# Longer loads in slots that shrink: an adaptive max-pool that streams 134 MB through one core

## The chip, the cores and the metric

One core of one Trainium2 chip. The metric is the device time of one execution in microseconds, as a median of several; executions of this kernel agree within about 0.2%. Every kernel was compared with the kernel before on the same chip in the same rounds; the experiments ran on four chips, on which the kernel before took 335.85 to 335.92 us. Two other kernels set side by side may have run on different chips. On one core a run is called slow when it lies more than 1.5% above the fastest run of the same kernel; comparisons below use fast runs. The granted clock was 1.0, and TensorE is not used.

## The reference

The input is 32 x 256 rows of 4,096 float32 values; each output is the maximum of 16 neighbouring values, 256 outputs per row.

```python
batch, channels, length = 32, 256, 4096
for i in range(output_size):                 # output_size = 256
    start = int(i * length / output_size)
    end = int((i + 1) * length / output_size)
    result[:, :, i] = np.max(x[:, :, start:end], axis=-1)
```

So 134.2 MB are read and 8.4 MB written, with one comparison per element. Since 4,096 is a multiple of 256, all windows have W = 16 elements (64 bytes), and the whole input is one row of windows, 16,384 of them for each of the 128 partitions.

## The kernel before

Loads go in turn through three slots of 760 windows (48,640 bytes per partition). VectorE reduces each slot into an output tile that stays in SBUF. Only after the last load has been issued are the outputs stored, in three DMAs. The 16,384 windows of a partition are cut in two groups so that the first group's outputs can be stored while the last inputs are still being reduced.

```python
SLOTS = 3
CHUNK = 760
GROUPS = [10 * CHUNK, total - 10 * CHUNK]     # 7,600 and 8,784 windows
CUT = 10 * CHUNK
ring = pool.tile([P, SLOTS, CHUNK * W], fp32, tag="ring", name="ring")
outs = [pool.tile([P, n], fp32, ...) for i, n in enumerate(GROUPS)]   # cut
for g, n in enumerate(GROUPS):
    # cut: xg, og are this group's views of input and output
    for a in range(0, n, CHUNK):
        b = min(a + CHUNK, n)
        slot = ring[:, n_loads % SLOTS, 0 : (b - a) * W]
        n_loads += 1
        nc.sync.dma_start(out=slot, in_=xg[:, a * W : b * W])
        nc.vector.reduce_max(
            out=outs[g][:, a:b],
            in_=slot.rearrange("p (n w) -> p n w", w=W),
            axis=mybir.AxisListType.X,
        )
    # cut: stores of group 0 in one piece, of group 1 in two, cut at CUT
for dst, src in stores:
    nc.sync.dma_start(out=dst, in_=src)
```

Of the kernel before, what the change touches and what calls it, by code (L numbers as in the profile page):

```python
# [1 line left out]

# [4 lines left out]


@with_exitstack
def kernel(  # L10
    ctx: ExitStack,
    tc: tile.TileContext,
    x: bass.AP,
    output_size: bass.AP,
    out: bass.AP,
):




    nc = tc.nc
    P = nc.NUM_PARTITIONS
    fp32 = mybir.dt.float32

    B, C, L = x.shape
    O = int(output_size)
    assert L % O == 0, (L, O)
    W = L // O
    total = B * C * O // P

    SLOTS = 3
    CHUNK = 760
    GROUPS = [10 * CHUNK, total - 10 * CHUNK]
    CUT = 10 * CHUNK
    assert sum(GROUPS) == total and B * C * O % P == 0

    pool = ctx.enter_context(tc.tile_pool(name="pool", bufs=1))
    ring = pool.tile([P, SLOTS, CHUNK * W], fp32, tag="ring", name="ring")
    outs = [
        pool.tile([P, n], fp32, tag=f"out{i}", name=f"out{i}")  # L40
        for i, n in enumerate(GROUPS)
    ]

    xw = x.flatten_outer_dims().rearrange("r (o w) -> (r o) w", w=W)
    ow = out.flatten_outer_dims().rearrange("r o -> (r o)")

    stores = []
    n_loads = 0
    first = 0
    for g, n in enumerate(GROUPS):  # L50
        xg = xw[first : first + P * n].rearrange("(p n) w -> p (n w)", p=P)
        og = ow[first : first + P * n].rearrange("(p n) -> p n", p=P)
        first += P * n
        for a in range(0, n, CHUNK):
            b = min(a + CHUNK, n)
            slot = ring[:, n_loads % SLOTS, 0 : (b - a) * W]
            n_loads += 1
            nc.sync.dma_start(out=slot, in_=xg[:, a * W : b * W])  # L58
            nc.vector.reduce_max(  # L59
                out=outs[g][:, a:b],  # L60
                in_=slot.rearrange("p (n w) -> p n w", w=W),
                axis=mybir.AxisListType.X,
            )
        if g < len(GROUPS) - 1:
            stores.append((og, outs[g]))
        else:
            for a, b in ((0, CUT), (CUT, n)):
                stores.append((og[:, a:b], outs[g][:, a:b]))

    for dst, src in stores:  # L70
        nc.sync.dma_start(out=dst, in_=src)


# [1 line left out]
_INS = ['x', 'output_size']  # L75
_OUTS = [((32, 256, 256), 'float32')]

_NUMBERS = {'output_size': 256}


# [26 lines left out]
```

## Time and profile before

| before | value |
|---|---|
| time, median of 6 runs (range) | 335.86 us (335.66 to 336.07) |
| loads: number, bytes per partition | 21 of 48,640 and 1 of 27,136 |
| period of the loads | 14.38 us |
| one reduction of 760 windows | 12.82 us |
| share of time that the 16 DMA engines are busy | 99.1% |

From the page of the kernel before: the span, the busy time of the engines, the packets and the DMA queue (packets, MB, share of 16 engines' span).

```profile
span 334.0 us, 111 instructions
...
DVE 276.3 (83%) x22; POOL 0.2 (0%) x4
...
DMA packets 3600, 142.61 MB, mean 427 GB/s; under 512 B 400, under 2 KB 400, under 8 KB 528
...
q1 hardware_dynamic: 3600, 142.61, 99.1%
```

VectorE (DVE) is busy for 83% of the time and the DMA engines for 99%. The second number has no room left in it. The timeline shows it from VectorE's side (start, duration, engine, instruction, and in brackets the idle time before it and what ended that):

```profile
61.14 12.82 DVE L59 TENSOR_REDUCE out<-ring 128x760 f32<-128x12160 f32 x1 [1.57 <-DMA ring<-in_x_dram]
75.53 12.82 DVE L59 TENSOR_REDUCE out<-ring 128x760 f32<-128x12160 f32 x1 [1.57 <-DMA ring<-in_x_dram]
89.91 12.82 DVE L59 TENSOR_REDUCE out<-ring 128x760 f32<-128x12160 f32 x1 [1.56 <-DMA ring<-in_x_dram]
```

VectorE works 12.82 us and waits 1.57 us, and every round of the two is 14.38 us. The trace also records each packet: one partition's row of a load is one packet, 48,640 bytes most often in 1.796 us, and each of the 16 engines carries 8 of the 128 rows: 8 x 1.796 = 14.37 us. So a load begins when the one before it ends. The sequencer that issues the loads (SP) waits long for VectorE, in its own view of waits (who waited for whom: total us, times, longest):

```profile
SPq L58 <- DVE out L59: 243.6, 19, 12.8
SPq L58 <- DMA ring<-in_x_dram: 37.2, 19, 15.9
```

That wait is not a loss: while SP waits for a slot, two other loads are still queued at the DMA engines.

### The profile page before, as it was taken

The numbers are of one execution on the slowest core, as the hardware profiler recorded it, in microseconds if no ns is written. First come the engines' busy times: TensorE is split into PE (matmuls) and PEld (weight loads), VectorE is DVE, ScalarE is ACT, GpSimd is POOL, SyncE is SP. The second block draws the span as 40 slices with busy tenths as digits, with TensorE's granted clock in tenths as the row PEclk, the third lists the DMA queues.
The fourth block names the chain that finished last, engine by engine and source line by source line (L and its number), as shares of the span: only waits on it lengthen the run. The fifth ranks groups of instructions, "written<-read, shape, count | busy, mean of one in ns | idle before, by whom it ended". The sixth has DMA issues, their size and how long they took to land.

```text
span 334.0 us, 111 instructions
## 1 busy us (share of the span) xinstructions
DVE 276.3 (83%) x22; POOL 0.2 (0%) x4
## 2 busy tenths in 40 slices
DVE  0088989889898988989898898988989898898990
POOL 0000000000000000000000000000000000000000
DMA  9999899999999999999998999999999999989997
GB/s 361 390 460 454 384 466 437 402 466 437 402 460 425 419 454 408 443 454 396 454 454 384 466 437 402 466 419 419 460 414 431 454 408 443 454 384 440 443 419 306
DMA packets 3600, 142.61 MB, mean 427 GB/s; under 512 B 400, under 2 KB 400, under 8 KB 528
## 3 DMA queue, kind: packets, MB, share of 16 engines
q1 hardware_dynamic: 3600, 142.61, 99.1%
HBM read 134.22 MB, written 8.39 MB: 427 GB/s over the span
## 4 chain that ended last, share of the span: by engine, by line
DMA 68%; DVE 27%; DVEq 2%; SPq 0%; issue 0%
DMA ring<-in_x_dram 68%; DVE out L59 27%; DVEq L102 2%; SPq L58 0%
## 5 line engine op out<-in xcount | busy, mean ns | idle before, releaser
L59 DVE TENSOR_REDUCE out<-ring 128x760 f32<-128x12160 f32 (+1 forms) x22 | 276.3, 12565 | 49.2 <-DMA ring<-in_x_dram 49.2
L88 POOL MEMSET const-bfloat16-1.0<- 128x1 bf16 x1 | 0.1, 101 | 0.0
L88 POOL MEMSET const-uint8-127<- 128x1 uint8 x1 | 0.1, 101 | 0.0
L88 POOL MEMSET const-float32-0.0<- 128x1 f32 x1 | 0.1, 98 | 0.2 <-issue 0.2
L88 POOL MEMSET const-float32-1.0<- 128x1 f32 x1 | 0.1, 98 | 0.0
## 6 DMA issues: line engine op xcount, KB each, us to landing
ring<-in_x_dram SPq DMA_DIRECT2D x21, 6080.0 KB, 30.3
out_dram<-out SPq DMA_DIRECT2D x2, 3800.0 KB, 30.1
ring<-in_x_dram SPq DMA_DIRECT2D x1, 3392.0 KB, 23.9
out_dram<-out SPq DMA_DIRECT2D x1, 592.0 KB, 7.6
```

Of the source, the lines that this page charges most:

```text
L59: nc.vector.reduce_max(out=outs[g][:, a:b], in_=slot.rearrange("p (n w) -> p n w", w=W), axis=mybir.AxisListType.X,)
L88: nc = _bacc.Bacc("TRN2", target_bir_lowering=False, num_devices=1)
L102: with _tile.TileContext(nc) as tc:
```

## The change

The intent is to use all of SBUF at every moment. At the start few outputs exist, so the three slots can be 64 KB per partition; as outputs accumulate, growing down from the top of one common area, the slots shrink round by round to 48 KB. This makes 19 loads of 22, each as long as memory and a cap of 64 KB per partition permit. Each group is loaded from its end backwards.

```diff
-    CHUNK = 760
-    GROUPS = [10 * CHUNK, total - 10 * CHUNK]
+    AREA = 53200
+    MOST = 65536 // (4 * W)
+    ALIGN = 4
+    ROUNDS_A = 3
+    LAST = 4
+    sizes = []
+    left = total
+    while left:
+        room = AREA - (total - left)
+        n = min(room // (SLOTS * W + SLOTS) // ALIGN * ALIGN, MOST)
+        for _ in range(SLOTS):
+            n = min(n, left)
+            if n:
+                sizes.append(n)
+                left -= n
+    groups = [sizes[: ROUNDS_A * SLOTS], sizes[ROUNDS_A * SLOTS :]]
...
-            slot = ring[:, n_loads % SLOTS, 0 : (b - a) * W]
+            at = n_loads % SLOTS * sizes[n_loads // SLOTS * SLOTS] * W
+            slot = area[:, at : at + size * W]
             nc.sync.dma_start(out=slot, in_=xg[:, a * W : b * W])
             nc.vector.reduce_max(
-                out=outs[g][:, a:b],
+                out=area[:, base + a : base + b],
...
-            for a, b in ((0, CUT), (CUT, n)):
-                stores.append((og[:, a:b], outs[g][:, a:b]))
+            end = sum(loads[len(loads) - LAST :])
+            for a, b in ((end, n), (0, end)):
+                stores.append((og[:, a:b], area[:, base + a : base + b]))
```

The loads become three each of 1,024, 980, 924, 868, 816 and 768 windows and one of 244.

More of the change, by code (lines that the diff above doesn't have):

```diff
@@ L29 @@
     total = B * C * O // P
+    assert B * C * O % P == 0
+    AREA = 53200
     SLOTS = 3
-    CHUNK = 760
-    GROUPS = [10 * CHUNK, total - 10 * CHUNK]
-    CUT = 10 * CHUNK
-    assert sum(GROUPS) == total and B * C * O % P == 0
-    pool = ctx.enter_context(tc.tile_pool(name="pool", bufs=1))
-    ring = pool.tile([P, SLOTS, CHUNK * W], fp32, tag="ring", name="ring")
-    outs = [
-        pool.tile([P, n], fp32, tag=f"out{i}", name=f"out{i}")
-        for i, n in enumerate(GROUPS)
-    ]
+    MOST = 65536 // (4 * W)
[13 more added lines that the diff above has]
+    groups = [sizes[: ROUNDS_A * SLOTS], sizes[ROUNDS_A * SLOTS :]]
+    pool = ctx.enter_context(tc.tile_pool(name="pool", bufs=1))
+    area = pool.tile([P, AREA], fp32, tag="area", name="area")
     xw = x.flatten_outer_dims().rearrange("r (o w) -> (r o) w", w=W)
@@ L49 @@
     first = 0
-    for g, n in enumerate(GROUPS):
+    low = AREA
+    for g, loads in enumerate(groups):
+        n = sum(loads)
         xg = xw[first : first + P * n].rearrange("(p n) w -> p (n w)", p=P)
@@ L53 @@
         first += P * n
-        for a in range(0, n, CHUNK):
-            b = min(a + CHUNK, n)
-            slot = ring[:, n_loads % SLOTS, 0 : (b - a) * W]
-            n_loads += 1
+        base = low - n
+        b = n
+        for i, size in enumerate(loads):
+            a = b - size
+            at = n_loads % SLOTS * sizes[n_loads // SLOTS * SLOTS] * W
+            slot = area[:, at : at + size * W]
             nc.sync.dma_start(out=slot, in_=xg[:, a * W : b * W])
             nc.vector.reduce_max(
-                out=outs[g][:, a:b],
+                out=area[:, base + a : base + b],
                 in_=slot.rearrange("p (n w) -> p n w", w=W),
@@ L63 @@
             )
-        if g < len(GROUPS) - 1:
-            stores.append((og, outs[g]))
-        else:
-            for a, b in ((0, CUT), (CUT, n)):
-                stores.append((og[:, a:b], outs[g][:, a:b]))
+            n_loads += 1
+            b = a
+        low = base
+        if g == 0:
+            stores.append((og, area[:, base : base + n]))
+        else:
+            end = sum(loads[len(loads) - LAST :])
+            for a, b in ((end, n), (0, end)):
+                stores.append((og[:, a:b], area[:, base + a : base + b]))
     for dst, src in stores:
```

## The prediction

> # Prediction
>
> **What bounds the kernel now.** The 16 DMA engines, from end to end. The page shows one queue keeping them busy for 99.1% of a 334.0 us span: 142.61 MB at 427 GB/s. VectorE is busy 276.3 us (83%); after each 12.82 us reduction it waits 1.56 us for a load, and loads come every 14.38 us (timeline). The trace's packet records show no gap over 0.03 us on any engine from the first load's packet (2.0 us into the span) to the last store's (1.1 us before its end). A row of a load is one packet: 48,640 bytes take 1.796 us, and 8 per engine make 14.37 us, the loads' period. So VectorE's 49.2 us of idle time (waits) costs nothing, nor do the 243.6 us that load issues wait for slots (the queue's own waits): two more loads are always queued.
>
> **What the change moves.** Bytes stay: 134.22 MB in, 8.39 MB out. The order view of the builds shows 22 loads becoming 19 (three each of 65,536, 62,720, 59,136, 55,552, 52,224 and 49,152 bytes per partition, one of 15,616). Data packets per engine fall from 200 to 176, if a 64 KB row stays one packet, and semaphore packets (9 ns each) from 25 to 22.
>
> **Cost of a packet.** 27,136 bytes take 1.009 us and 48,640 bytes 1.796 us: 36.6 ns per 1,000 bytes and 13.5 ns fixed, of which 3 ns overlap the next packet. Estimate from these: 24 x 10.6 ns + 3 x 9 ns = 0.28 us saved. A 64 KB packet should take 2.41 us, its load 19.3 us, the reduction of 1,024 windows 17.3 us (12.82 x 1024/760), so VectorE keeps up and the queue stays fed.
>
> The Trainium skill, "DMA: Bandwidth & Descriptors", section "Anatomy of one DMA", fits about 2.0 us of fixed cost to every DMA. Paid here, three loads fewer would save 6 us. This trace disagrees: a period of 14.38 us against 14.37 us of packets leaves 0.01 us per load; a queued DMA hides its fixed part behind its predecessor.
>
> **Ends.** The first load must still begin at 2.0 us; its first packets took 2.3 to 3.1 us instead of 1.8, and I expect a similar extra. The last store grows from 0.6 to 1.3 MB and waits for the last reduction. Estimate: the last 768-window load lands at 309 us, its reduction ends at 322, the 244-window one (4.1 us) at 326; the store's packets are ready at 327.5, while the two stores ahead (10.4 and 6.0 us) keep the engines busy until 330. Slack 2 us, so no bubble. The last two stores' rows no longer begin at multiples of 64 bytes: 0 to 0.2 us.
>
> **Prediction: 335.6 us**, range 335.0 to 336.2: within 2% (0.985), faster 0.003, slower 0.012. Larger loads gain about 0.1%, as the pipe was already full.
>
> **What would show each step.** DMA share of 99% again; 3,168 packets (2,432 for loads, 384 for stores, 352 for semaphores); 64 KB packets at 2.41 us; VectorE waiting 2 us per load in the first rounds, 1.5 in the last; VectorE busy within 0.5 us of 276; no DMA gap before the last store.
>
> **What would make it wrong.** A 65,536-byte row cut in two (+0.1 us at most) or moved at another rate; loads waiting for a later reduction than the third back, since slots now overlap at shifted places, so that the queue runs dry at round changes; a drained queue before the last store (some 2 us); unaligned store rows at a multiple of their time (stores carry 19 us per engine, so 10% is 2 us).

## The result, and the profile after

| | before | after |
|---|---|---|
| time, median of 6 runs (range) | 335.86 us (335.66 to 336.07) | 335.67 us (335.42 to 335.87) |
| ratio of the fast runs | | 0.9993, interval 0.998 to 1.0006 |
| time, repeated on another occasion (9 and 5 runs) | 335.86 us (335.64 to 336.1) | 335.53 us (335.42 to 335.77) |

A ratio is the mean time of one kernel's fast runs over that of the other's in the same rounds, so it is not quite the ratio of the medians in the table. The time lies inside the predicted range of 335.0 to 336.2 us and 0.07 us from the predicted 335.6. The change makes no difference that these intervals can tell from none; both pairs of medians lean the same way, by 0.19 and 0.33 us.

The page after:

```profile
span 333.9 us, 109 instructions
...
DVE 276.0 (83%) x19; POOL 0.2 (0%) x4
...
DMA packets 3168, 142.61 MB, mean 427 GB/s; under 512 B 352, under 2 KB 352, under 8 KB 352
...
q1 hardware_dynamic: 3168, 142.61, 99.1%
```

There are 432 packets fewer and the same bytes, the same share and the same rate. A 64 KB row is one packet (3,168 = 19 x 128 + 3 x 128 for data and 22 x 16 for semaphores). The timeline after, over a change of round:

```profile
42.33 17.22 DVE L75 TENSOR_REDUCE area<-area 128x1024 f32<-128x16384 f32 x1 [2.13 <-DMA area<-in_x_dram]
61.68 17.22 DVE L75 TENSOR_REDUCE area<-area 128x1024 f32<-128x16384 f32 x1 [2.13 <-DMA area<-in_x_dram]
80.28 16.49 DVE L75 TENSOR_REDUCE area<-area 128x980 f32<-128x15680 f32 x1 [1.38 <-DMA area<-in_x_dram]
98.72 16.49 DVE L75 TENSOR_REDUCE area<-area 128x980 f32<-128x15680 f32 x1 [1.96 <-DMA area<-in_x_dram]
```

Everything is stretched in proportion: the period is 19.35 us (8 packets of 2.418 us), the reduction 17.22 us. The first wait of a new round is shorter (1.38 us) only because a shorter load follows a longer reduction; no later slot is waited for. SP's waits:

```profile
SPq L74 <- DVE area L75: 246.2, 16, 17.2
SPq L74 <- DMA area<-in_x_dram: 38.8, 16, 20.9
```

Three loads fewer, and in total nearly the same waiting as before (285.0 us against 280.8 us). It is still not on the path.

### The profile page after: what moved, and what is told of

The parts are those of the page before. It is cut to its first block, busy times and chain, and to the rows that moved or that the text cites. A ratio compares the mean times of both kernels' runs of the same rounds, so it can differ in the third digit from the quotient of the medians.

```text
span 333.9 us, 109 instructions
## 1 busy us (share of the span) xinstructions
DVE 276.0 (83%) x19; POOL 0.2 (0%) x4
## 2 busy tenths in 40 slices
DMA packets 3168, 142.61 MB, mean 427 GB/s; under 512 B 352, under 2 KB 352, under 8 KB 352
## 3 DMA queue, kind: packets, MB, share of 16 engines
q1 hardware_dynamic: 3168, 142.61, 99.1%
## 4 chain that ended last, share of the span: by engine, by line
DMA 63%; DVE 34%; another core or an unknown queue 1%; issue 0%; SPq 0%
DMA area<-in_x_dram 63%; DVE area L75 34%; SPq L74 0%
## 5 line engine op out<-in xcount | busy, mean ns | idle before, releaser
L75 DVE TENSOR_REDUCE area<-area 128x1024 f32<-128x16384 f32 (+6 forms) x19 | 276.0, 14525 | 50.0 <-DMA area<-in_x_dram 50.0
```

What stands on the lines that cost most here:

```text
L75: nc.vector.reduce_max(out=area[:, base + a : base + b], in_=slot.rearrange("p (n w) -> p n w", w=W), axis=mybir.AxisListType.X,)
```

## The experiments

The theory: the 16 DMA engines move bytes without a pause, so the size and number of loads count only through a few nanoseconds per packet; whatever a DMA costs besides is hidden behind the DMA ahead of it in the queue. Rivals: each DMA has an exposed cost of microseconds, which another loss happened to cancel; VectorE shares the bound; the end of the kernel or the shifted slots gave back a gain.

Results agreed with the reference except in the two kernels that are wrong on purpose.

### Smaller loads, three slots: more DMAs and more packets

```diff
-    CHUNK = 760
-    GROUPS = [10 * CHUNK, total - 10 * CHUNK]
-    CUT = 10 * CHUNK
+    CHUNK = 190
+    GROUPS = [40 * CHUNK, total - 40 * CHUNK]
+    CUT = 40 * CHUNK
```

> The kernel before with loads a quarter as long: 87 loads of at most 12,160 bytes per partition instead of 22, still three slots. Theory (the queue never drains; a packet costs 10.6 ns beside its bytes, a load only its 9 ns semaphore packet): packets per engine 696 + 24 instead of 176 + 24, so 520 x 10.6 ns + 65 x 9 ns = 6.1 us more, 342.0 us; DMA share stays at 99%. Rival (each DMA pays about 2 us): 65 x 2 us more, about 466 us, with DMA share near 70%.

Measured: 342.44 and 345.52 us in the fast runs, 350.11 and 350.70 in two that count as slow; the kernel before 335.9. The profiled run is one of the slow ones, with its packets and queue:

```profile
DMA packets 12962, 142.63 MB, mean 409 GB/s; under 512 B 1440, under 2 KB 1440, under 8 KB 1696
...
q1 hardware_dynamic: 12960, 142.61, 98.7%
```

The exposed 2 us per DMA are refuted: 130 us did not come. But the theory's 342.0 us was hit only by the fastest run, and executions that differ by 8 us mean that something other than packets varied. The packet records of the profiled (slow) run show gaps of up to 2 us on single DMA engines. (The kept records don't name the engine of a packet; here and below they are joined, end to start, into 16 chains.) That called for two separations: packets from DMAs, and DMAs from the depth of the queue.

### As many packets, no more DMAs

The 22 loads of before, but each partition's part is gathered from four pieces (Q = 4) of 12,160 bytes; outputs and stores follow the same order (cut here).

```diff
-        xg = xw[first : first + P * n].rearrange("(p n) w -> p (n w)", p=P)
+        xg = xw[first : first + P * n].rearrange("(p q n) w -> p q (n w)", p=P, q=Q)
...
-            nc.sync.dma_start(out=slot, in_=xg[:, a * W : b * W])
+            nc.sync.dma_start(
+                out=slot.rearrange("p (q e) -> p q e", q=Q),
+                in_=xg[:, :, a // Q * W : b // Q * W],
+            )
...
```

> The kernel before with its 22 loads, but each partition's part of a load is gathered from four pieces of 12,160 bytes, so that there are as many packets as in the quarter loads and no more loads. Packets per engine: 704 for loads and 72 for stores (two stores come in pieces) instead of 176 and 24. Theory (packets cost, loads do not): 576 x 10.6 ns = 6.1 us more, 342.0 us, equal to the quarter loads within 0.5 us. Rival (the number of DMAs costs): 336 us, as before.

Measured: 338.22 us (338.12 to 338.38) against 335.9. The page:

```profile
DMA packets 12816, 142.61 MB, mean 424 GB/s; under 512 B 400, under 2 KB 912, under 8 KB 1936
...
q1 hardware_dynamic: 12816, 142.61, 99.6%
```

Packets do cost something, 2.3 us for 576 more per engine, but that is 4.0 ns each and not the 10.6 ns of the prediction. And this kernel was not equal to the quarter loads, so those lost their further time elsewhere.

### Smaller loads, six slots

```diff
-    SLOTS = 3
+    SLOTS = 6
     CHUNK = 190
```

> The quarter loads (12,160 bytes per partition, 87 loads) with six slots instead of three. With three slots they varied from 342.4 to 350.7 us, with gaps on single DMA engines; the quarter rows, which never drained, showed only 4 ns per extra packet (2.3 us for 576). Theory (the excess over that was the queue running dry, as two loads of 3.6 us do not cover 3.3 us of reduction, 1.2 to 2.3 us from issue to packet and 1 us between the first and the last engine): with five loads queued 520 x 4 ns + 65 x 9 ns = 2.7 us over the kernel before, 338.6 us, all runs within 0.5 us, no engine gaps. Rival (each of 65 more loads costs 0.1 to 0.2 us whatever is queued): 342 to 350 us as with three slots.

Measured: 339.0 us (338.93 to 339.19) against 335.85. The queue of this kernel:

```profile
DMA packets 12962, 142.63 MB, mean 423 GB/s; under 512 B 1440, under 2 KB 1440, under 8 KB 1696
...
q1 hardware_dynamic: 12960, 142.61, 99.6%
```

With three more slots and nothing else changed, the scatter vanished and the engines were busy 99.6% of the time. So 65 more loads with 520 more packets cost 3.15 us (0.4 us more than expected), which is 0.05 us per load, packets included; after 65 x 9 ns for semaphore packets, 4.9 ns remain per packet. What the three-slot version lost beyond that came from its shallow queue, since depth alone cured it. Its slow profile shows the loss in two forms: per engine 3.0 us of gaps, and 10.1 us by which packets exceed the median time of their size (1.5 us with six slots). Few of those long packets follow a gap, so the gaps alone don't explain the loss. (The two versions ran on different chips, on which the kernel before took 335.9 and 335.85 us.)

### Half the work on VectorE

```diff
-                in_=slot.rearrange("p (n w) -> p n w", w=W),
+                in_=slot.rearrange("p (n w) -> p n w", w=W)[:, :, : W // 2],
```

> The changed kernel with each reduction reading only the first 8 of 16 elements of every window (a wrong result on purpose): VectorE's work halves to about 139 us, the DMAs stay. Theory (DMA engines bound everything): 335.7 us as the changed kernel, within 0.3 us. Rival (VectorE, 83% busy and 34% of the chain that ended last, shares the bound): a gain of several us.

Measured: 335.65 us (335.47 to 335.70) against 335.9, with

```profile
DVE 139.4 (42%) x19; POOL 0.2 (0%) x4
...
q1 hardware_dynamic: 3168, 142.61, 99.1%
```

VectorE's work halved and the time stayed that of the changed kernel. VectorE bounds nothing, although in the page of the changed kernel the chain that ended last gives it 34% of the span.

### Two slots of 64 KB: a candidate that failed

If only bytes and packets count, two slots are enough, and every load can be 64 KB.

```diff
-    SLOTS = 3
-    CHUNK = 760
+    SLOTS = 2
+    CHUNK = 1024
+    TAIL = 252
...
```

Cut: the last load gets a piece of SBUF of its own, and the groups and stores are cut to match.

> A candidate: 15 loads of 64 KB, one of 772 windows and one of 252 in a piece of its own, in only two slots. 17 loads, packets per engine 136 + 24 (200 before, 176 in the changed kernel). Theory: a slot is free 17.2 us after its load lands and the first packet follows its issue by about 1.0 us (0.73 to 1.75 us at the start), together 18.3 us, less than the 19.35 us that the other load takes: queue stays fed, 40 fewer packets than before: 335.86 - 0.45 = 335.4 us, DMA share 99%. Rival (three slots are needed, or DMAs have an exposed cost of about 2 us): a gap of 0.5 to 1 us at each of 14 loads, 343 to 350 us.

Measured: 353.39 us (350.73 to 354.07) against 335.9: slower than the rival expected, and my theory's number failed by 18 us. The timeline:

```profile
42.57 17.22 DVE L64 TENSOR_REDUCE out<-ring 128x1024 f32<-128x16384 f32 x1 [2.33 <-DMA ring<-in_x_dram]
64.00 17.22 DVE L64 TENSOR_REDUCE out<-ring 128x1024 f32<-128x16384 f32 x1 [4.22 <-DMA ring<-in_x_dram]
83.77 17.22 DVE L64 TENSOR_REDUCE out<-ring 128x1024 f32<-128x16384 f32 x1 [2.54 <-DMA ring<-in_x_dram]
104.76 17.22 DVE L64 TENSOR_REDUCE out<-ring 128x1024 f32<-128x16384 f32 x1 [3.77 <-DMA ring<-in_x_dram]
```

```profile
q1 hardware_dynamic: 2880, 142.61, 96.4%
```

VectorE now waits 2.3 to 4.4 us where the changed kernel had 2.13 us at this size, and the DMA share fell. I had allowed 1.0 us from issue to first packet and had left out two things that the packet records show. First, the 16 engines do not work in step: from the first engine's semaphore to the last one's, a load lands over 0.8 us at the start of this run and a median of 2.2 us over all of it. A load counts as landed when the slowest engine is done, while the fast ones already run dry. Second, while other packets are moving, the first packet on an engine that ran dry comes a median of 2.2 us after the issue in this run; and it takes a median of 0.56 us longer than its size demands. Per engine the gaps sum to 7.5 us, and what all packets take above the median of their size sums to 9.7 us (0.85 us in the kernel before): together most of the 17.5 us lost. The packets right after a gap make only about 3.5 us of the 9.7; why others ran long too was not found.

### The same two slots, freed earlier

The two-slot kernel with the halved reduction of above, so that only the moment changes at which a slot becomes free.

```diff
 # on the two-slot kernel
-                in_=slot.rearrange("p (n w) -> p n w", w=W),
+                in_=slot.rearrange("p (n w) -> p n w", w=W)[:, :, : W // 2],
```

> The two-slot kernel with 64 KB loads (353.4 us), each reduction reading half of every window (wrong result on purpose), so that a slot is free after about 8.7 us instead of 17.2 us; DMAs the same. Theory (the two-slot kernel ran dry because the next load was issued too late): the queue is fed again, 335.5 us, DMA share 99%, landing spread of the engines stays near 0.8 us. Rival (two slots or 17 loads of 64 KB are slow by themselves, in the memory or the engines): stays near 353 us.

Measured: 335.61 us (335.49 to 335.75) against 335.85; the landing spread stayed at 0.8 to 0.9 us.

```profile
197.19 8.69 DVE L64 TENSOR_REDUCE out<-ring 128x1024 f32<-128x8192 f32 x1 [10.66 <-DMA ring<-in_x_dram]
216.54 8.69 DVE L64 TENSOR_REDUCE out<-ring 128x1024 f32<-128x8192 f32 x1 [10.66 <-DMA ring<-in_x_dram]
```

The period is 19.35 us again. So neither two slots nor 64 KB rows are slow; the late issue was.

### Two slots of 48 KB

```diff
-    SLOTS = 3
+    SLOTS = 2
     CHUNK = 760
```

> The kernel before with two slots instead of three: 22 loads of 48 KB. Asks what the size of a load is worth when only one load is queued behind the one that moves. In the two-slot kernel with 64 KB loads each load came 1.0 to 1.3 us late (353.4 us, 14 loads with a wait), the spread of the engines rose to 2 us and packets came a median of 2.2 us after their issue. Theory (fed only if the other load's time covers reduction, issue to packet and spread): slack is 14.38 - 12.84 - 2.2 - 0.95 = -1.6 us, against 19.35 - 17.24 - 2.2 - 0.8 = -0.9 us with 64 KB, at 20 loads instead of 14: about 1.5 to 2 us per load, 365 to 375 us. Rival (a late load costs the same few tenths whatever its size, or two slots suffice at 48 KB): under 353 us.

Measured: 355.13 and 357.25 us in the fast runs, 363.21 and 364.08 in the slow ones, against 335.92. The estimate of 365 to 375 us was too high and the rival's bound too low. In the middle of the timeline (138 to 242 us) only every second load is late: VectorE waits 2.7 to 3.2 us, then 1.6 to 1.9.

```profile
152.71 12.82 DVE L59 TENSOR_REDUCE out<-ring 128x760 f32<-128x12160 f32 x1 [1.56 <-DMA ring<-in_x_dram]
168.41 12.82 DVE L59 TENSOR_REDUCE out<-ring 128x760 f32<-128x12160 f32 x1 [2.89 <-DMA ring<-in_x_dram]
```

I had not modelled that. Nor did the 2.2 us that I took over from the last kernel hold: here the first packet on an engine that ran dry came a median of 1.2 us after the issue, though in most rounds all 16 engines were still moving packets when the load was issued. With a queue this shallow, 64 KB loads (median 353.39 us, on another occasion) were better than 48 KB ones by 2 to 4 us in fast runs. The direction is that of the change's intent, but the size is small, and these two kernels scatter too much to say more.

### One slot: what a load costs when nothing hides it

The kernel before, and the quarter loads, each with `SLOTS = 1`.

> The kernel before with one slot: every load waits for the reduction of the load before it, so what a load costs apart from its bytes is laid bare. Estimate: 14.37 us of packets, 0.8 us of slow first packets, 12.82 us of reduction, 1.2 to 2.3 us from issue to packet, 0.3 us from packet to reduction, about 30 us per load, 660 us in all (640 to 680).

> One slot with the quarter loads: same bytes, 65 more loads, all of them exposed. If a load that nothing hides costs 2.0 us beside bytes and reduction, 65 x 2.0 + 8.3 us (reductions) + 2.7 us (packets) over the one-slot kernel, about 800 us; with slow first packets and the spread of the engines counted, about 2.7 us per load, 845 us. With a queue that is fed the same 65 loads cost at most 3 us (six slots).

Measured: 655.99 and 826.72 us (two executions each). One round of each, first with 48 KB loads, then with 12 KB:

```profile
47.96 12.82 DVE L59 TENSOR_REDUCE out<-ring 128x760 f32<-128x12160 f32 x1 [17.06 <-DMA ring<-in_x_dram]
78.13 12.82 DVE L59 TENSOR_REDUCE out<-ring 128x760 f32<-128x12160 f32 x1 [17.35 <-DMA ring<-in_x_dram]
```

```profile
25.78 3.32 DVE L59 TENSOR_REDUCE out<-ring 128x190 f32<-128x3040 f32 x1 [6.07 <-DMA ring<-in_x_dram]
35.16 3.32 DVE L59 TENSOR_REDUCE out<-ring 128x190 f32<-128x3040 f32 x1 [6.07 <-DMA ring<-in_x_dram]
```

A load of 14.37 us of packets keeps VectorE waiting 17.2 us, one of 3.6 us keeps it waiting 6.1 us: some 2.4 to 2.8 us per load beside the bytes. From the totals: 170.7 us more, less 10.0 us of further VectorE work and about 2.3 us of packets (520 x 4.5 ns), over 65 loads, gives 2.4 us per load. So a cost of microseconds per DMA does exist. These 2.4 us hold everything that is exposed: a median of 1.1 us from issue to first packet, a first packet that runs 0.6 to 0.7 us long, and the wait for the last engine. With six slots the same 65 loads cost 0.05 us each.

### The end of the kernel: one store fewer

```diff
-            for a, b in ((end, n), (0, end)):
+            for a, b in ((0, n),):
```

> The changed kernel with its last two stores joined into one, which must wait for the last reduction (326.0 us in the trace of the changed kernel). The first store ends at 323.4 us, and the packets of the joined one come 1.2 to 2.3 us after 326.0, so that the engines idle 4 to 5 us. Theory (in the changed kernel the middle store covers the last reductions): 9.0 us of store from about 327.7 us, 340.0 us in all (339 to 341). Rival (the end is not sensitive; one DMA fewer): 335.6 us.

Measured: 339.19 us (339.04 to 339.22) against 335.86, and 335.53 for the changed kernel on the same chip. DMA share (the second-last column; the last is GB/s) in two stretches of the end, first the changed kernel, then this one:

```profile
300.00:323.00 23.00, 21.39 (x3) 0.00 (x0) 1.00 1.00 431
323.00:329.00 6.00, 3.00 (x1) 0.00 (x0) 1.00 0.96 411
```

```profile
300.00:323.00 23.00, 21.38 (x3) 0.00 (x0) 1.00 0.97 419
323.00:329.00 6.00, 2.77 (x1) 0.00 (x0) 1.00 0.49 208
```

The changed kernel keeps the engines moving while the last 768 and 244 windows are reduced, because the middle store was ready long before. Without it there is a gap of 3.5 to 4.4 us per engine, and the total is 3.7 us longer. The gap was half a microsecond shorter than I expected: with all engines idle the packets came 0.84 to 0.99 us after the issue, not 1.2 to 2.3.

### The changed kernel again

> The changed kernel itself, unaltered, five rounds against the kernel before on the same chip, to narrow the interval of the difference (0.19 us of medians in the first measurement, ratio 0.9993, interval 0.998 to 1.0006). Theory (24 fewer packets per engine at 4 to 5 ns and 3 fewer semaphore packets, less 0.1 us of slower first packets): 0 to 0.2 us faster. If packets saved 10.6 ns as the prediction had it, about 0.3 us faster.

Measured: 335.53 us (335.42 to 335.77) against 335.86 (335.64 to 336.1), ratio 0.9992, interval 0.9979 to 1.0006. This does not tell 0.1 from 0.3 us.

## Why the prediction was right

**The bound.** The prediction placed it in the DMA engines. Halving VectorE's work left the time where it was, and removing the cover of the middle store, hence idling the engines for 3.5 to 4.4 us, cost 3.3 us over the kernel before. A rate within a packet can be read off two sizes: 36,480 bytes lie between the 455 ns of 12,160 bytes and the 1,796 ns of 48,640, which is 36.76 ns per 1,000 bytes, or 27.2 GB/s per engine and about 435 GB/s for 16. The Trainium skill, "DMA: Bandwidth & Descriptors", section "Where 436 GB/s comes from", derives 435.2 GB/s. A rival would be a limit that the engines share, such as the memory; packets should then be shorter when few engines move. They are not: in the one-slot quarter loads 95 packets of 12,160 bytes have at most eight packets moving at their middle, and their median is 455 ns too. So the limit is that of each engine or its own path. At this rate 142.61 MB take 327.7 us. The remaining 6.3 us of the 334 us span are an estimate by parts: 1.74 us before the first packet, 1.3 us after the last, 0.9 us of packets longer than their size's median (above all the first of the run), about 1.6 us of packet overhead, and 0.8 us in which some engines have begun or ended and others not. No size of load touches most of these.

**The 2 us per DMA.** The 2 us of the rivals come from the Trainium skill, "DMA: Bandwidth & Descriptors", section "Anatomy of one DMA". The section fits its 2.0 us to DMAs issued from GpSimd, and all DMAs here are issued from SP. The prediction set the figure aside: the period of the loads left only 0.01 us over the packets. The experiments show both sides: 2.4 us per load when nothing else is queued, and 0.05 us, packets included, with a fed queue. A cost of microseconds exists as latency and is not paid as throughput.

**The cost of a packet was mis-sized.** The prediction took 13.5 ns fixed, less 3 ns of overlap, from the 27,136-byte and 48,640-byte packets. Two neighbouring sizes whose times scatter by a few ns are a poor base for an intercept. The four times smaller rows gave 4.0 ns and the six-slot kernel 4.9 ns. So the 24 packets save 0.1 us, not 0.25. The first packets of the run, which the prediction expected to exceed their size by as much as before, did so: 0.73 us on average before, 0.90 and 0.66 us in the two profiles of the changed kernel. An engine that starts earlier mostly has the longer first packet, and the mean of start plus excess is 2.69 us before and 2.76 and 2.71 us after. Summed per engine, packet time fell from 330.91 us to 330.79 and 330.56 us. The sum of the prediction, 0.28 us, lies within what the two measurements scatter over (0.19 and 0.33 us), but that agreement is luck as far as the size goes and decides nothing: the predicted range of 335.0 to 336.2 us also holds the time of the kernel before.

**The ends.** The last 768-window load was reduced from 308.8 us (predicted 309), the last reduction ended at 326.0 us, the middle store at 329.4 us (330). With 0.9 us from issue to packet, the last store's packets were ready 1.5 us before the first engine was free for them, at 328.4 us: no gap, as predicted. The prediction's 2.0 us before the first packet was a misreading; it is 1.74 us in both kernels. The rows that do not begin at multiples of 64 bytes cost nothing visible: 10,192 bytes took 387 ns, 12 ns over the wire rate, and the aligned rows of 35,136 bytes took 1,304 ns, also 12 ns over.

**The shifted slots.** Feared in the prediction, they did no harm: each load waits for the third reduction back, and with three slots of 64 KB there are 2 x 19.35 us of queued loads against 17.2 us of reduction and 2 to 3 us of latency.

**What stays open.** The time from issue to first packet after an idle spell was seen, not explained: a median of 2.2 us with two slots of 64 KB, 1.2 us with two of 48 KB, 1.1 us with one slot, where all engines are idle, and 0.9 us for the last store. Nor is it explained why many packets ran long in the kernels with a shallow queue. Whether the change is worth 0.1 or 0.3 us is below what was measured. No correct kernel that was tried beat the changed one.

## What to carry to other kernels

Ask first whether the DMA queue ever runs dry: if the engines are busy from the first load to the last store, longer loads buy only a few ns per packet saved, and faster compute does not change the time. What must be covered is the last engine's landing, plus the computation on the slot, plus the time from issue to packet, and the loads already queued have to be longer than that sum with a margin of microseconds, not tenths; depth in slots and size of loads both pay for it, and depth did so more cheaply here (six slots of 12 KB: 339.0 us; two of 64 KB: 353.4 us, on another chip). At the end, keep a store that is already complete between the last load and the store that waits for the last result.

## What the Trainium skill lacked or had wrong

- "DMA: Bandwidth & Descriptors", section "Anatomy of one DMA", fits 2.0 us of fixed cost per DMA to DMAs issued from GpSimd; no page read has such a fit for DMAs issued from SP. Measured here, from SP: 2.4 us per load with one slot, 0.05 us per load (8 packets per engine included) with six. The page's rules say that the setup overlaps when a DMA is issued early; they do not say that the fit must not be summed over queued DMAs.
- The same page, section "Measured", has 341 GB/s for a DMA of 1 MB issued from GpSimd, and does not say whether others were queued. Loads of 1.6 MB from SP, six deep, reached a mean of 423 GB/s over the whole span here, loads of 6 MB three deep 427.
- The same page, section "Where 436 GB/s comes from", says that the HBM side (about 358 GB/s) binds HBM to SBUF transfers; the condition that both cores of the pair stream stands elsewhere on the page and not there. With one core running it did not bind: mean 427 GB/s, 27.2 GB/s per engine within a packet. (The page "HBM Reference", section "Specifications (TRN2)", gives about 425 GB/s for a core streaming alone, which this trace agrees with.)
- No page read has the restart cost of a load: after an idle spell the first packet on an engine took a median of 0.56 us (two slots of 64 KB) to 0.73 us (one slot of 48 KB) longer, but only 0.09 us in the three-slot quarter loads; the last store's first packets took no longer (one last store).
- None of them has a figure for how far apart the engines finish one load: 0.95 us from first to last engine in the kernel before, unchanged from the first load to the last, 0.99 and 0.64 us in the two profiles of the changed kernel, and a median of 2.2 us in the two-slot kernel with 64 KB loads, whose queue runs dry.
- None of them has the time from issue to first packet on an engine that ran dry behind other loads: a median of 2.2 us with two slots of 64 KB and 1.2 us with two of 48 KB.
